# Depthwise convolution taps of a decoder trunk as 32-column products in four column tiles, with host-laid parameters

## The chip, the core and the metric

The kernel runs on one core of one Trainium2 chip. The metric is the time of one execution of the whole program in device microseconds, given as the median of several runs. Before the change it is 1438.3 us (three runs, 1434.78 to 1441.6).

## The reference, cut to what matters

The program is a decoder trunk of four pre-norm residual layers over 256 tokens and 1024 channels, in float32. The token mixer of layer i is attention (layers 0 and 3), a convolution module (layer 1) or a gated recurrence (layer 2). Each layer then has a SwiGLU feed-forward block and a gate by a per-layer embedding p. The change touches the convolution module and the handling of p:

```python
def _conformer_conv(u, w_pw1, b_pw1, w_dw, b_dw, ln_g, ln_b, w_pw2, b_pw2):
    a = u @ w_pw1 + b_pw1                               # 1024 -> 2048
    a = a[..., :CONV_CH] * jax.nn.sigmoid(a[..., CONV_CH:])
    a = causal_depthwise_conv(a, w_dw) + b_dw           # 31 taps, each channel alone
    a = jax.nn.silu(_layernorm(a, ln_g, ln_b))          # over the channels
    return a @ w_pw2 + b_pw2
...
        gate = jax.nn.sigmoid(_rmsnorm(h, ple_norm_g[i]) @ ple_w_gate[i])
        h = h + (p[i] @ ple_w_proj[i]) * gate
```

## The kernel before, in words

A large product has its float32 operands cut into a high and a low part, so it is three products in a reduced float32 type (lines 187 to 189, `mm`). Weights arrive in granules of 128 x 1024 elements (`granule`): a DMA of SyncE's queue fills one of 4 `raw` buffers (line 163), ScalarE writes the high part into one of 9 `whi` buffers (line 166), and VectorE the low part into one of 8 `wlo` buffers (line 167). A scheduler orders the instructions of every engine when the program is built, by the order in which the code names them and by its own estimates; on the chip each queue then runs in that fixed order, SyncE's queue of DMAs too. `issue_after` pins a few instructions behind others.

The convolution (`conv`) holds the channels in eight groups of 128 partitions, with the 256 tokens along the free axis. For each group, pw1 makes 48 products of 256 columns into an `acc` bank, ScalarE takes the sigmoid (line 765), and VectorE the gated product into the tile `glu` (line 768), with 30 zeros ahead of the tokens. The taps then run on two engines. Groups 0 to 4 are chains on VectorE, one instruction for a tap, each reading `glu` shifted by one token and adding to `co` (line 720). Groups 5 to 7 are products on TensorE: for each tap ScalarE scales the identity by the tap's 128 weights (`diag`, line 734), and one float32 product of this 128 x 128 matrix with the shifted `glu` adds to a `mm` bank (line 735). A float32 product shows as two records in the trace, here two of 256 columns.

The statistics are kept relative to `base`, an estimate of the mean from groups 0 and 1. It is subtracted on VectorE, or on TensorE by a product with minus the identity (lines 787 and 796). `moments` (line 751) sums `co` and its square over the channels by products with two columns. When the last group is in, a short chain on VectorE makes 1 / sigma, four products spread it over the partitions (line 822), and each group is normalised, passed through Silu and split into the operand `yT` (lines 830 to 832, 209 and 210). pw2 (`linear`) takes its weights in two halves of 512 columns.

p of each layer is read in two tiles (`pin`), transposed on TensorE and split (`embed_setup`, by `split_T`, line 222), some time before it is needed. `embed` multiplies it by its weights. `conv_setup` reads the convolution's parameters as rows and transposes them on TensorE (lines 680 and 683).

The recurrence of layer 2 holds another use of small tiles: line 970 makes products whose stationary side has 32 or 64 columns, so that their outputs lie in 32 or 64 partitions. With 32 columns the products come in turns for output partitions 0 to 31 and 64 to 95.

Of the kernel before, what the change touches and what calls it, by code (L numbers as in the profile page):

```python
# [16 lines left out]
AF = mybir.ActivationFunctionType  # L17
# [14 lines left out]
TAPS = 31  # L32


def parts(x, n, bits=12):
# [77 lines left out]
class Trunk:  # L113
# [41 lines left out]
    def granule(self, src, nk, n):  # L155
        """src: list of (dram AP [nk*128, cols], first column); hi and lo parts [128, nk, n]"""
# [13 lines left out]
    def ktiles(self, w, cols):  # L170
        """k-tiles (hi, lo) of w[:, cols], where cols: list of (first, count), 256 or 512 in all"""
# [12 lines left out]
    def mm(self, ps, x, w, start, stop):  # L184
        """ps += x.T @ w, float32 operands in two parts each: (hi, lo)"""
# [5 lines left out]
    def mms(self, ps, xs, ws, between=None):  # L191
        """ps = sum of x.T @ w; between() is placed among the products"""
# [10 lines left out]
    def cut(self, x, t, k0=0, k1=None):  # L203
        """k-tiles of an operand for the tokens of tile t (None: all)"""
# [8 lines left out]
    def split_T(self, src, x, k, t):  # L213
        """src [128 tokens of tile t, nk*128] -> k-tiles k.. of the operand x"""
# [13 lines left out]
    def rsqrt(self, ss, scale, w=1):  # L228
        """1 / sqrt(ss * scale + EPS) of [128, w] by Newton's iteration"""
# [24 lines left out]
    def gain(self, row, n=D):  # L254
        """a row of DRAM on all partitions"""
# [31 lines left out]

    def residual(self, t, c, ps):
# [7 lines left out]
    def ffn(self, i, norm, done, pre):  # L296
# [3 lines left out]
        with self.scope(self.nm("ffn")) as pool:  # L300
# [34 lines left out]
            for j in range(NJ):  # L335
# [4 lines left out]
                if j == 5 and i == 0:  # L340
                    self.embed_setup(1)
                    self.embed_setup(2)
                if j == 5 and i == 1:
                    self.embed_setup(3)
# [15 lines left out]
    def embed_setup(self, i):  # L360
        """p transposed and split"""
        pT = self.pT[i] = self.operand(2, "pT", 4)
        for t in range(NT):
            pt = self.tmp("pin", [P, 256], 2)
            self.nc.sync.dma_start(pt, self.a["p"][i, 0, t * P : (t + 1) * P])
            self.split_T(pt, pT, 0, t)
# [42 lines left out]
    def mla_setup(self):  # L409
        """the rotary tables [128, tile, 32]: cos | cos and -sin | sin"""  # L410
# [9 lines left out]
        with self.scope("rope") as pool:  # L420
# [18 lines left out]
            def rounded(x, unit):  # L439
                """x to a multiple of unit (a power of two)"""  # L440
# [53 lines left out]
    def rope(self, x, t, pool):  # L494
        """in place on x [128 tokens, heads, 32]"""
# [14 lines left out]
    def mla(self, i, norm, done, pre):  # L510
# [8 lines left out]
        with self.scope(self.nm("mla")) as pool:  # L519
# [38 lines left out]
            def heads(gi):  # L558
                """q^T, k^T [96, 4, 256], v of four heads"""
# [83 lines left out]
            for gi in range(NH // HG):  # L643
                cur = heads(gi)
                if i == 0 and gi == 0:
                    self.embed_setup(0)
# [13 lines left out]
    def conv_setup(self):  # L660
        nc = self.nc
        a = self.a
        C = self.const
        self.cpar = C.tile([P, KD, TAPS + 3], F32, name="cpar")
        self.cb1 = C.tile([P, 2 * KD], F32, name="cb1")
        self.mean = C.tile([P, P], F32, name="mean")
# [3 lines left out]
        with self.scope("cpar") as pool:  # L670
            rows = self.tmp("rows", [TAPS + 3, D], 1, pool=pool)
            nc.sync.dma_start(rows[:TAPS], a["conv_w_dw"][0])
            for r, k in enumerate(("conv_b_dw", "conv_ln_g", "conv_ln_b")):
                nc.sync.dma_start(rows[TAPS + r : TAPS + r + 1], a[k])
            b1 = self.tmp("b1", [2 * KD, P], 1, pool=pool)
            nc.sync.dma_start(b1, a["conv_b_pw1"][0].rearrange("(c p) -> c p", p=P))
            pt = self.bank("tr", 2)
            n = TAPS + 3
            for c in range(KD):
                nc.tensor.transpose(pt[:, c * n : (c + 1) * n], rows[:, c * P : (c + 1) * P], self.ident[:n, :n])  # L680
            nc.vector.tensor_copy(self.cpar, pt[:, : KD * n].rearrange("p (c n) -> p c n", n=n))
            pt = self.bank("tr", 2)
            nc.tensor.transpose(pt[:, : 2 * KD], b1, self.ident[: 2 * KD, : 2 * KD])
            nc.vector.tensor_copy(self.cb1, pt[:, : 2 * KD])
# [6 lines left out]
    def conv(self, i, norm, done, pre):  # L691
        nc = self.nc
# [3 lines left out]
        PAD = TAPS - 1  # L696
        BASE = 2
        with self.scope(self.nm("conv")) as pool:
# [7 lines left out]
            neg = tmp("neg", [P, P], 1)  # L706
            nc.gpsimd.tensor_scalar(out=neg, in0=self.ident, scalar1=-1.0, scalar2=None, op0=ALU.mult)
# [3 lines left out]
            nc.tensor.matmul(stat[:, : 4 * NT], self.ones, zero, start=True, stop=False)  # L711

            def taps_dve(groups, start):
                """chains of taps; those of a group take turns"""
                for cs in groups:
                    for c, k in cs:
                        if k == 0:
                            start(c)
                        else:
                            V.scalar_tensor_tensor(out=co[:, c], in0=xin[c][:, k : k + S], scalar=par(c, k), in1=co[:, c], op0=ALU.mult, op1=ALU.add)  # L720

            def first(c):
                V.tensor_scalar(out=co[:, c], in0=xin[c][:, :S], scalar1=par(c, 0), scalar2=par(c, TAPS), op0=ALU.mult, op1=ALU.add)

            def first_shifted(c):
                nc.gpsimd.tensor_scalar(out=co[:, c], in0=base, scalar1=-1.0, scalar2=par(c, TAPS), op0=ALU.mult, op1=ALU.add)
                V.scalar_tensor_tensor(out=co[:, c], in0=xin[c][:, :S], scalar=par(c, 0), in1=co[:, c], op0=ALU.mult, op1=ALU.add)

            def taps_pe(c, ps, ks):
                """one diagonal product for each tap"""  # L730
                for k in ks:
                    d = tmp("diag", [P, P], 16)
                    with self.behind():
                        nc.scalar.activation(d, self.ident, AF.Copy, scale=par(c, k))
                    nc.tensor.matmul(ps, d, xin[c][:, k : k + S], start=k == 0, stop=False)  # L735

            def square(c, src, bias=0.0):
                sq[c] = tmp("work", [P, S], 5)
                return nc.scalar.activation(sq[c], src, AF.Square, bias=bias)

            def evict(c, ps):
                nc.scalar.activation(co[:, c], ps, AF.Identity, bias=par(c, TAPS))
                square(c, ps, par(c, TAPS))

            def moments(c):
                """sums over the channels of co (less base) and of its square"""
# [7 lines left out]
            sq = {}  # L754
            xin = []
            for c0 in range(0, KD, 2):
                ws = self.conv_head(i, c0) if c0 else self.head
                for cc in range(2):
                    c = c0 + cc
                    ps = self.acc()  # L760
# [5 lines left out]
                    x = tmp("glu", [P, PAD + S], KD)  # L766
                    nc.gpsimd.memset(x[:, :PAD], 0.0)
                    V.scalar_tensor_tensor(out=x[:, PAD:], in0=ps[:, :S], scalar=self.cb1[:, c : c + 1], in1=sg, op0=ALU.add, op1=ALU.mult)
                    xin.append(x)
            lead = 6  # L770
            taps_dve([[(c, k) for c in (0, 1)] for k in range(TAPS)], first)
            taps_dve([[(2, k)] for k in range(lead)], first)
            pe = {5: self.bank("mm", 2)[:, :S]}
            taps_pe(5, pe[5], range(20))
# [5 lines left out]
            for c in (0, 1):  # L780
# [302 lines left out]
```

## Time and profile before

| | |
|---|---|
| median of three runs | 1438.3 us |
| lowest, highest | 1434.78, 1441.6 us |
| the profiled execution: first to last instruction (span) | 1432.0 us |
| mean granted TensorE clock | 0.991 of full |
| busy share of the span: TensorE, VectorE, ScalarE | 97%, 65%, 51% |
| DMA: bytes, mean rate | 228.90 MB, 160 GB/s |

The profiled execution's own time in the metric is not listed; only its span is. The median of the runs lies 6.3 us over the span: that is what lies around the instructions. In the rows, PE is TensorE's products, PEld its weight loads, DVE VectorE, ACT ScalarE and SPq SyncE's queue. A name like `mm<-glu,diag` says what is written from what.

### The profile page before, as it was taken

The page shows a single profiled execution, that of the slowest core. Times are in us where ns is not written, and L with a number is a line of the kernel's source. Part 1 is how long each engine was busy: PE and PEld are TensorE (multiplying, and loading weights), DVE is VectorE, ACT ScalarE, POOL GpSimd, SP SyncE. Part 2 cuts the span into 40 slices and gives each one's busy share as a digit, 9 for nine tenths or more (in the row PEclk, how much of TensorE's full clock was granted, in tenths as well). Part 3 has the DMA queues.
Part 4 walks back from the last instruction along what each step waited for, and adds up shares of the span by engine and source line. Part 5 has one row for each costly group of instructions (what it writes and reads, how often), then busy time and mean ns, then how long its engine had stood idle before and what let it go on. Part 6 is the DMA issues. An engine that isn't in the chain of part 4 may idle for free.

```text
span 1432.0 us, 19941 instructions
## 1 busy us (share of the span) xinstructions
PE 1382.2 (97%) x7102; PEld 1142.4 (80%) x7102; DVE 933.5 (65%) x1812; ACT 734.0 (51%) x1259; POOL 24.8 (2%) x50
## 2 busy tenths in 40 slices
PE   6999999998999999999989999999999999999996
PEld 5787887876998788888778887887878887788885
DVE  7866555558798865554867767655558867555556
ACT  6665444446655654443554445544445655544443
POOL 0000000001000000000000000000000100000000
PEclk9999999999899999999999999999999999999999
DMA  7433665635630365564573342755535522655532
GB/s 241 167 98 118 200 195 184 194 116 193 213 109 1 120 219 176 180 194 156 160 223 118 124 157 95 240 186 184 191 121 176 195 74 94 209 192 192 186 124 77
DMA packets 172873, 228.90 MB, mean 160 GB/s; under 512 B 11284, under 2 KB 135748, under 8 KB 172774
## 3 DMA queue, kind: packets, MB, share of 16 engines
q1 hardware_dynamic: 172774, 227.63, 49.5%
q8 instruction: 56, 0.92, 0.3%
q14 instruction: 43, 0.35, 0.1%
HBM read 226.53 MB, written 1.05 MB: 159 GB/s over the span
## 4 chain that ended last, share of the span: by engine, by line
PE 75%; DMA 9%; DVE 7%; ACT 6%; issue 3%; SPq 0%; ACTq 0%; DVEq 0%
PE mm L187 12%; PE mm L188 12%; PE mm L189 12%; PE acc L188 8%; PE acc L187 8%; PE acc L189 8%; DMA raw<-in_ffn_w_down_dram 4%; PE tr L222 3%; DVE wlo L167 3%; ACT whi L166 3%; PE mm L735 3%; DMA raw<-in_ple_w_gate_dram 2%; PE acc L957 1%; DMA raw<-in_mla_w_uq_dram 1%; PE acc L604 1%
## 5 line engine op out<-in xcount | busy, mean ns | idle before, releaser
L167 DVE TENSOR_TENSOR wlo<-raw,whi 128x1024 fp32r<-128x1024 f32 (+2 forms) x420 | 498.4, 1200 | 148.9 <-ACT whi L166 105.5
L166 ACT ACTIVATE whi<-raw 128x1024 fp32r<-128x1024 f32 (+2 forms) x420 | 426.8, 1040 | 258.4 <-DMA raw<-in_ffn_w_down_dram 88.6
L187 PE MATMUL mm<-whi,xT 128*128 128x512 f32 x816 | 328.9, 403 | 0.7 <-ACT xT L209 0.4
L189 PE MATMUL mm<-whi,xT 128*128 128x512 f32 x816 | 322.1, 395 | 0.0
L188 PE MATMUL mm<-wlo,xT 128*128 128x512 f32 x816 | 321.7, 394 | 0.0
L189 PEld LDWEIGHTS mm<-whi,xT 128*128 128x128 f32 x816 | 153.5, 188 | 32.7 <-DVE xT L210 0.8
L187 PEld LDWEIGHTS mm<-whi,xT 128*128 128x128 f32 x816 | 153.8, 188 | 30.3 <-ACT xT L209 0.9
L188 PEld LDWEIGHTS mm<-wlo,xT 128*128 128x128 f32 x816 | 153.9, 189 | 28.5
L187 PE MATMUL acc<-whi,aT 128*128 128x512 f32 x352 | 138.7, 394 | 0.6 <-ACT aT L209 0.6
L188 PE MATMUL acc<-wlo,aT 128*128 128x512 f32 x352 | 138.6, 394 | 0.0
L189 PE MATMUL acc<-whi,aT 128*128 128x512 f32 x352 | 136.4, 389 | 0.5 <-DVE aT L210 0.5
L315 DVE SCALAR_TENSOR_TENSOR ga<-mm,rs_y,sg 128x256 f32<-128x256 f32 x88 | 42.3, 481 | 139.0 <-ACT sg L313 139.0
L313 ACT ACTIVATE sg<-mm,rs_y 128x256 f32<-128x256 f32 x88 | 41.0, 465 | 136.6 <-PE mm L189 136.6
L187 PE MATMUL acc<-whi,xT 128*128 128x512 f32 (+2 forms) x272 | 102.2, 380 | 2.2 <-ACT xT L209 1.4
L189 PE MATMUL acc<-whi,xT 128*128 128x512 f32 (+2 forms) x272 | 102.6, 379 | 0.2 <-DVE xT L210 0.2
L188 PE MATMUL acc<-wlo,xT 128*128 128x512 f32 (+2 forms) x272 | 102.2, 377 | 0.0
L187 PEld LDWEIGHTS acc<-whi,aT 128*128 128x128 f32 x352 | 66.1, 188 | 17.5 <-ACT aT L209 3.3
L189 PEld LDWEIGHTS acc<-whi,aT 128*128 128x128 f32 x352 | 66.0, 188 | 16.5 <-DVE aT L210 1.7
L188 PEld LDWEIGHTS acc<-wlo,aT 128*128 128x128 f32 x352 | 66.2, 188 | 13.0
L210 DVE TENSOR_TENSOR aT<-tr,aT 128x256 fp32r<-128x256 f32 x88 | 37.3, 424 | 57.7 <-ACT aT L209 57.7
L720 DVE SCALAR_TENSOR_TENSOR co<-glu,cpar,co 128x256 f32<-128x256 f32 x150 | 60.7, 477 | 0.1
L187 PEld LDWEIGHTS acc<-whi,xT 128*128 128x128 f32 x272 | 51.0, 189 | 11.6 <-ACT xT L209 2.4
(271 smaller groups left out, 1902.4 us busy)
## 6 DMA issues: line engine op xcount, KB each, us to landing
raw<-in_ffn_w_gu_dram SPq DMA_DIRECT2D x352, 256.0 KB, 4.3
raw<-in_ffn_w_down_dram SPq DMA_DIRECT2D x88, 512.0 KB, 4.2
raw<-in_ple_w_gate_dram SPq DMA_DIRECT2D x32, 512.0 KB, 5.2
raw<-in_hgrn_w_in_dram SPq DMA_DIRECT2D x64, 256.0 KB, 4.0
raw<-in_mla_w_out_dram SPq DMA_DIRECT2D x16, 512.0 KB, 4.4
raw<-in_conv_w_pw_dram SPq DMA_DIRECT2D x32, 256.0 KB, 4.8
raw<-in_mla_w_in_dram SPq DMA_DIRECT2D x16, 336.0 KB, 3.4
raw<-in_mla_w_uq_dram SPq DMA_DIRECT2D x12, 384.0 KB, 4.2
```

The lines of the kernel that those rows point to most:

```text
L166: nc.scalar.activation(hi[:, :used], raw[:, :used], AF.Copy)
L167: nc.vector.tensor_tensor(out=lo[:, :used], in0=raw[:, :used], in1=hi[:, :used].bitcast(F32), op=ALU.subtract)
L187: mm(ps, x[0], w[0], start=start, stop=False)
L188: mm(ps, x[0], w[1], start=False, stop=False)
L189: return mm(ps, x[1], w[0], start=False, stop=stop)
L210: v = self.nc.vector.tensor_tensor(out=lo, in0=src, in1=hi.bitcast(F32), op=ALU.subtract)
L222: nc.tensor.transpose(pt[:, (i - k0) * P : (i - k0 + 1) * P], src[:, i * P : (i + 1) * P], self.ident)
L313: nc.scalar.activation(sg, ps[:, :256], AF.Silu, scale=r)
L315: nc.vector.scalar_tensor_tensor(out=ga, in0=ps[:, 256:], scalar=r, in1=sg, op0=ALU.mult, op1=ALU.mult)
L604: nc.tensor.matmul(s1[:, hh], qT[:HD, h, P:], kT[:HD, h], start=True, stop=False)
L720: V.scalar_tensor_tensor(out=co[:, c], in0=xin[c][:, k : k + S], scalar=par(c, k), in1=co[:, c], op0=ALU.mult, op1=ALU.add)
L735: nc.tensor.matmul(ps, d, xin[c][:, k : k + S], start=k == 0, stop=False)
```

## The change

The host lays out four more inputs: p transposed, the convolution's parameters with the channel on the partition, pw1's bias in the same way, and `conv_taps`. Groups 2 and 3 stay chains on VectorE. For the six other groups a group of 128 channels is cut into four blocks j of 32. Four DMAs (`spread`) copy block j of `glu`, SBUF to SBUF, into `win[:, j]`, where a partition is one of 32 channels at one of 4 shifts. A matrix of 128 x 32 with the four taps on its diagonals then does four taps of 32 channels in one product of 256 columns, and its output goes to partitions 32j to 32j+31. Eight steps cover 31 taps, so a group takes 32 products, the four blocks in turns within a step. The matrices come by DMA (`tap_weights`, 512 KB for a group). `win` has three buffers, `tapw` two. The `diag` and `neg` work is gone. pw2 takes its weights by rows of 128 x 1024 (`linear_rows`), five of them named before the last tap groups. p is loaded and split where `embed_weights` is called, which now takes one `raw` buffer more.

```diff
     def embed_weights(self, i):
+        pT = self.pT[i] = self.operand(2, "pT", 2)
+        raw = self.tmp("raw", [P, 1024], 4, pool=self.wpool)[:, : 2 * S].rearrange("p (k n) -> p k n", k=2)
+        self.nc.sync.dma_start(raw, self.a["p_t"][i].rearrange("(k p) n -> p k n", p=P))
+        with self.behind():
+            self.split(*pT, raw)
...
+            def spread(c):
+                win[c] = tmp("win", [P, QUAD, WIN], 3)
+                for j in range(QUAD):
+                    src = xin[c][32 * j : 32 * j + 32]
+                    shifts = bass.AP(tensor=src.tensor, offset=src.offset, ap=[src.ap[0], [1, QUAD], [1, WIN]])
+                    nc.sync.dma_start(win[c][:, j], shifts)
+            def tap_weights(c):
+                tapw[c] = tmp("tapw", [P, QUAD, STEPS, 32], 2)
+                nc.sync.dma_start(tapw[c], a["conv_taps"][:, c])
+            def taps_pe(c):
+                ps = self.bank("mm", 2)[:, :S]
+                for m in range(STEPS):
+                    for j in range(QUAD):
+                        nc.tensor.matmul(
+                            ps[32 * j : 32 * j + 32], tapw[c][:, j, m], win[c][:, j, QUAD * m : QUAD * m + S],
+                            start=m == 0, stop=m == STEPS - 1,
+                        )
+                return ps
...
             for c0 in range(0, KD, 2):
...
+                    if c not in CHAINS:
+                        tap_weights(c)
...
+                    if c not in CHAINS:
+                        spread(c)
+                if c0 == 4:
+                    for c in range(BASE):
+                        nc.scalar.activation(co[:, c], taps_pe(c), AF.Identity, bias=par(c, TAPS))
...
+            for k in range(TAPS):
+                for c in CHAINS:
...
+            self.embed_weights(2)
+            rows = lambda k: self.granule([(a["conv_w_pw2"][0][k * P : (k + 1) * P], 0)], 1, D)
+            ws = [rows(k) for k in range(5)]
+            for c in CHAINS:
+                V.tensor_tensor(out=co[:, c], in0=co[:, c], in1=base, op=ALU.subtract)
+                square(c)
+                moments(c)
+            for c in range(4, KD):
+                V.scalar_tensor_tensor(out=co[:, c], in0=taps_pe(c), scalar=par(c, TAPS), in1=base, op0=ALU.add, op1=ALU.subtract)
+                fence = [square(c).ins]
+                fence.append(moments(c).ins)
...
+    def linear_rows(self, x, ws, use, done, pre):
+        pick = lambda w, c: tuple(y[:, 0, c * 512 : (c + 1) * 512] for y in w)
+        xs = [self.cut(x, t) for t in range(NT)]
+        ps = [self.acc() for c in range(2)]
+        for k in range(KD):
+            for c in range(2):
+                self.mm(ps[c], xs[0][k], pick(ws[k], c), k == 0, k == KD - 1)
...
```

## Rows read from the trace of the kernel before

**Rows 1.** The page: the span, and busy time, share of the span and instructions of two engines.
```profile
span 1432.0 us, 19941 instructions
...
PE 1382.2 (97%) x7102; PEld 1142.4 (80%) x7102; DVE 933.5 (65%) x1812; ACT 734.0 (51%) x1259; POOL 24.8 (2%) x50
```

**Rows 2.** The page: the chain that ended last, share of the span by engine.
```profile
PE 75%; DMA 9%; DVE 7%; ACT 6%; issue 3%; SPq 0%; ACTq 0%; DVEq 0%
```

**Rows 3.** Busy time of each engine in four stretches of the convolution: pw1, taps, statistics, pw2. The numbers behind a stretch are its length, then busy time and records of each engine; after POOL stand the granted clock, the DMA share and GB/s.
```profile
363.00:411.70 48.70, 48.68 (x386) 48.70 (x386) 42.86 (x84) 24.77 (x41) 0.46 (x1) 0.94 0.45 146
411.70:464.00 52.30, 51.74 (x264) 45.52 (x263) 45.04 (x103) 36.12 (x93) 1.51 (x2) 0.97 0.19 61
464.00:474.30 10.30, 9.27 (x36) 6.78 (x36) 7.22 (x32) 4.53 (x10) 0.00 (x0) 0.83 0.01 2
474.30:498.40 24.10, 24.10 (x110) 19.30 (x111) 22.26 (x52) 15.51 (x28) 0.43 (x2) 1.00 0.45 141
```

**Rows 4.** The chain of waits from 411 us on, in order of time: start, us, what (x records).
```profile
411.74 8.64 PE mm L735 x40
...
421.24 8.21 PE mm L735 x38
...
429.87 3.46 PE mm L735 x16
...
435.90 8.27 PE mm L735 x30
444.17 0.43 PE mm L796 x2
444.61 6.91 PE mm L735 x32
...
452.30 6.59 PE mm L735 x30
...
459.36 0.48 ACT co L742
459.88 3.88 PE tr L751 x32
```

**Rows 5.** Line 970 with 32 columns, in stretches of 20 to 35 ns: length, busy time and, in brackets, the records of that line in flight in the stretch; then clock, DMA share and GB/s.
```profile
792.41:792.43 0.02, 0.01 (x2) 1.00 0.25 77
792.43:792.47 0.03, 0.03 (x2) 1.00 0.46 119
792.47:792.49 0.03, 0.03 (x4) 1.00 0.49 123
792.49:792.52 0.03, 0.03 (x6) 1.00 0.66 171
792.52:792.55 0.03, 0.03 (x8) 1.00 0.69 205
```

**Rows 6.** The timeline of TensorE at line 970: start, us from the first start to the last end, line, what (stationary side 128*32 or 128*64), records.
```profile
792.42 0.45 PE L970 MATMUL acc<-qf,kb 128*32 128x32 f32 x16
...
792.80 0.50 PE L188 MATMUL mm<-wlo,xT 128*128 128x512 f32 x1
...
794.50 0.68 PE L970 MATMUL acc<-qf,kb 128*64 128x64 f32 x8
```

**Rows 7.** The timeline of VectorE: the gated product of group 3, taps in a row on two or three chains, and one low part.
```profile
390.06 0.48 DVE L768 SCALAR_TENSOR_TENSOR glu<-acc,cb,work 128x256 f32<-128x256 f32 x1
...
410.91 1.22 DVE L167 TENSOR_TENSOR wlo<-raw,whi 128x1024 fp32r<-128x1024 f32 x1
...
424.79 32.15 DVE L720 SCALAR_TENSOR_TENSOR co<-glu,cpar,co 128x256 f32<-128x256 f32 x81
```

**Rows 8.** The setup on TensorE: the transposes of p as a group, and the timeline around those of the parameters.
```profile
L222 PE MATMUL tr<-ident,pin x16: 270/272/328, 46.6 to 580.4; 128*128 128x128 f32 x16
...
46.65 0.44 PE L222 MATMUL tr<-ident,pin 128*128 128x128 f32 x2 [0.15 <-ACT xT L589]
...
163.51 0.39 PE L189 MATMUL acc<-whi,aT 128*128 128x512 f32 x1
163.83 0.68 PE L680 MATMUL tr<-ident,rows 34*128 34x34 f32 x8
...
164.60 0.50 PE L187 MATMUL mm<-whi,xT 128*128 128x512 f32 x1
```

**Rows 9.** The chain of waits from the gate of layer 0 into the convolution.
```profile
350.96 4.73 DMA raw<-in_conv_w_pw_dram
...
355.78 1.06 ACT whi L166
356.87 1.23 DVE wlo L167
```

**Rows 10.** DMA issues: what, records, KB each, median us from issue to landing; and one issue on SyncE's queue.
```profile
raw<-in_conv_w_pw_dram SPq DMA_DIRECT2D x8, 512.0 KB, 4.9
...
360.98 0.34 SPq L257 DMA_DIRECT2D gain<-in_norm_g_dram  x1
```

**Rows 11.** Around pw2: low parts of its second half, and the high parts of the feed-forward block's first weights.
```profile
476.66 4.62 DVE L167 TENSOR_TENSOR wlo<-raw,whi 128x1024 fp32r<-128x1024 f32 x4
...
490.23 3.89 ACT L166 ACTIVATE whi<-raw 128x1024 fp32r<-128x1024 f32 x4
```

More of the change, by code (lines that the diff above doesn't have):

```diff
@@ L32 @@
 TAPS = 31
+QUAD = 4
 def parts(x, n, bits=12):
@@ L286, in linear @@
         yield
+    def linear_rows(self, x, ws, use, done, pre):
[5 more added lines that the diff above has]
+                self.mm(ps[c], xs[0][k], pick(ws[k], c), k == 0, k == KD - 1)
+        for c in range(2):
+            use(0, c, ps[c])
+        done(0)
+        for c in range(2):
+            ps = self.acc()
+            for k in range(KD):
+                self.mm(ps, xs[1][k], pick(ws[k], c), k == 0, k == KD - 1)
+            use(1, c, ps)
+            del ps
+            if c == 0:
+                pre()
+        done(1)
     def residual(self, t, c, ps):
@@ L669, in conv_setup @@
         nc.gpsimd.memset(self.ones, 1.0)
[L670 to L684, printed above, removed]
     def conv_head(self, i, c0=0):
@@ L711, in conv @@
             nc.tensor.matmul(stat[:, : 4 * NT], self.ones, zero, start=True, stop=False)
[L713 to L735, printed above, removed]
@@ L737, in square @@
-            def square(c, src, bias=0.0):
+            xin, win, tapw, sq = [], {}, {}, {}
+            def spread(c):
[7 more added lines that the diff above has]
+                nc.sync.dma_start(tapw[c], a["conv_taps"][:, c])
@@ L738, in square @@
+            def taps_pe(c):
[7 more added lines that the diff above has]
+                return ps
+            def square(c):
                 sq[c] = tmp("work", [P, S], 5)
-                return nc.scalar.activation(sq[c], src, AF.Square, bias=bias)
@@ L765, in conv @@
                     nc.scalar.activation(sg, ps[:, S:], AF.Sigmoid, bias=self.cb1[:, KD + c : KD + c + 1])
-                    x = tmp("glu", [P, PAD + S], KD)
+                    x = tmp("glu", [P, PAD + S + 2], 4)
                     nc.gpsimd.memset(x[:, :PAD], 0.0)
-                    V.scalar_tensor_tensor(out=x[:, PAD:], in0=ps[:, :S], scalar=self.cb1[:, c : c + 1], in1=sg, op0=ALU.add, op1=ALU.mult)
+                    nc.gpsimd.memset(x[:, PAD + S :], 0.0)
+                    V.scalar_tensor_tensor(out=x[:, PAD : PAD + S], in0=ps[:, :S], scalar=self.cb1[:, c : c + 1], in1=sg, op0=ALU.add, op1=ALU.mult)
                     xin.append(x)
[L770 to L774, printed above, removed]
+                    if c not in CHAINS:
[3 more added lines that the diff above has]
+                        nc.scalar.activation(co[:, c], taps_pe(c), AF.Identity, bias=par(c, TAPS))
             pm = self.bank("tr", 2)[:, :S]
@@ L779, in conv @@
             V.tensor_scalar(out=base, in0=pm, scalar1=KD / BASE, scalar2=None, op0=ALU.mult)
-            for c in (0, 1):
+            for c in range(BASE):
                 V.tensor_tensor(out=co[:, c], in0=co[:, c], in1=base, op=ALU.subtract)
-            taps_pe(5, pe[5], range(20, TAPS))
-            for c in (6, 7):
-                pe[c] = self.bank("mm", 2)[:, :S]
-                taps_pe(c, pe[c], range(8))
-                if c == 6:
-                    nc.tensor.matmul(pe[5], neg, base, start=False, stop=True)
-                taps_pe(c, pe[c], range(8, 16))
-                if c == 6:
-                    for b in (0, 1):
-                        square(b, co[:, b])
-                        moments(b)
-                evict(c - 1, pe[c - 1])
-                moments(c - 1)
-                taps_pe(c, pe[c], range(16, TAPS))
-                nc.tensor.matmul(pe[c], neg, base, start=False, stop=True)
-            evict(7, pe[7])
-            moments(7)
-            order = [[(2, k + lead), (3, k), (4, k)] for k in range(TAPS)]
-            taps_dve([[(c, k) for c, k in g if k < TAPS] for g in order], first_shifted)
-            V.tensor_tensor(out=co[:, 2], in0=co[:, 2], in1=base, op=ALU.subtract)
-            for c in (2, 3, 4):
-                fence = [square(c, co[:, c]).ins]
+                square(c)
+                moments(c)
+            for k in range(TAPS):
+                for c in CHAINS:
+                    if k == 0:
+                        V.tensor_scalar(out=co[:, c], in0=xin[c][:, :S], scalar1=par(c, 0), scalar2=par(c, TAPS), op0=ALU.mult, op1=ALU.add)
+                    else:
+                        V.scalar_tensor_tensor(out=co[:, c], in0=xin[c][:, k : k + S], scalar=par(c, k), in1=co[:, c], op0=ALU.mult, op1=ALU.add)
+            self.embed_weights(2)
[3 more added lines that the diff above has]
+                V.tensor_tensor(out=co[:, c], in0=co[:, c], in1=base, op=ALU.subtract)
+                square(c)
+                moments(c)
+            for c in range(4, KD):
+                V.scalar_tensor_tensor(out=co[:, c], in0=taps_pe(c), scalar=par(c, TAPS), in1=base, op0=ALU.add, op1=ALU.subtract)
+                fence = [square(c).ins]
                 fence.append(moments(c).ins)
@@ L833, in conv @@
                 split = self.split(yT[0][:, c], yT[1][:, c], z)
-                if c == 3:
+                if c in (1, 3, 5):
                     self.fence = split
-                    ws.append(self.ktiles(a["conv_w_pw2"][0], [(512, 512)]))
-            next(self.linear(yT, ws, self.residual, done, pre))
+                    ws.append(rows(len(ws)))
+            self.linear_rows(yT, ws, self.residual, done, pre)
     def hgrn_setup(self):
@@ L1065, in run, with layouts @@
                 self.gate(i, n3, n1.do, lambda: None)
+def layouts(x):
+    w = x["conv_w_dw"][0]
+    steps = (TAPS + QUAD - 1) // QUAD
+    full = np.zeros((steps * QUAD, D), np.float32)
+    full[:TAPS] = w
+    full = full.reshape(steps, QUAD, KD, QUAD, 32)
+    taps = np.zeros((32, QUAD, KD, QUAD, steps, 32), np.float32)
+    for c in range(32):
+        taps[c, :, :, :, :, c] = full[:, :, :, :, c].transpose(1, 2, 3, 0)
+    par = np.concatenate([w, x["conv_b_dw"], x["conv_ln_g"], x["conv_ln_b"]])
+    return {
+        "p_t": np.ascontiguousarray(x["p"][:, 0].transpose(0, 2, 1)),
+        "conv_taps": taps.reshape(P, KD, QUAD, steps, 32),
+        "conv_par": np.ascontiguousarray(par.reshape(TAPS + 3, KD, P).transpose(2, 1, 0)),
+        "conv_b1": np.ascontiguousarray(x["conv_b_pw1"][0].reshape(2 * KD, P).T),
+    }
 def kernel(**inputs):
```

30 lines of the change are left out of this document (7 added, 23 removed).

## The prediction, made before the changed kernel ran

> **What bounds the kernel now.** Read the page's first part before all else: in a span of 1432.0 us TensorE is busy for 97%, VectorE for 65% [rows 1]. The chain that ended last agrees, with 75% of it on TensorE [rows 2]. Then go to the stage that the change rebuilds. In the stretches, pw1 (363.0 to 411.7) keeps TensorE busy for 48.68 of 48.70 us, the taps (411.7 to 464.0) for 51.74 of 52.30, the statistics for 9.27 of 10.30, pw2 for all of 24.10 [rows 3]. VectorE has 45.04 us of work in the tap stretch, so it is close to being a second bound there. The chain of waits through that stretch is almost nothing but line 735, the products with the diagonal matrices [rows 4]: 8.64 + 8.21 + 3.46 + 8.27 + 6.91 + 6.59 = 42.1 us for 186 records. So the convolution ends when TensorE's own work ends, and what counts is how much of that work the change takes away and whether it opens a wait.
>
> **The change part by part.** Durations are those of the profiled execution; the sum is made against its span, 1432.0, and the median of the runs lies 6.3 above it.
>
> Taps on TensorE, removed. The 42.1 us go. A record of 256 columns at full clock takes 8.21 / 38 = 0.216 us [rows 4], so 186 would need 40.2; the other 1.9 us are a piece at half clock (30 records there took 8.27). The three products with minus the identity go too, 3 x 0.43 = 1.3 [rows 4]. Together 43.4.
>
> Taps on TensorE, added. Six groups of 32 products are 192, or 384 records of 256 columns. One after another that is 384 x 0.216 = 82.9 us; with four column blocks side by side 96 x 0.216 = 20.7. Which of the two holds is the main question, and the trace has one place that speaks of it. At line 970 the products with 32 stationary columns lie by turns in two column blocks. Two records are in flight within the first 20 ns, and the count then grows by two every 30 ns or so: 2, 2, 4, 6, 8 [rows 5]. Sixteen records take 0.45 us [rows 6]; less about 0.2 for the last to end, that is 0.25 / 15 = 0.017 us for each. The 64-column products, which lie in one block only, take 0.68 us for eight, which gives (0.68 - 0.2) / 7 = 0.07 each [rows 6], so half as many columns in one block would be 0.035 each. Two blocks thus run fully beside each other. No row shows four, nor 256 columns. I take four, because the pairs start together, and keep both ends: 20.7 and 82.9.
>
> [...] A float32 product is two records on the same block. [...]
>
> Entering and leaving the narrow form costs something. The last pair of line 970 starts near 792.67 and the next wide product at 792.80 [rows 6], some 0.1 us after its columns are through. With both edges I take 0.2 for a group, 1.2 for six; 0 if the edges are free, 3.6 if the scheduler cuts each group into three. So the taps are 20.7 + 1.2 = 21.9 and the step saves 21.5 us.
>
> Taps on VectorE. 155 instructions become 62. In a row they start 32.15 / 81 = 0.397 us apart [rows 7], so the two chains are 24.6 us. Group 3 arrives at about 390.1 [rows 7], group 2 an eighth of pw1 (48.7 / 8 = 6.1) earlier. With the last low parts of pw1 (four, 4.62 [rows 11]), five gated products (2.0) and the work on `base` (1.3) the chains end near 384 + 32.5 = 416.5. Behind them stand seven low parts of the weights for p and pw2, 7 x 4.62 / 4 = 8.1, and only then perhaps the instruction that empties group 4's bank, near 426. TensorE is through with pw1 at 411.7, with groups 0 and 1 (7.3) and the mean at 419.8, and with 4 and 5 at 427. Both `mm` banks are then full, and VectorE comes just in time. I take no wait; 0 to 8.
>
> Waits that the change adds. The matrices of group 6 need the buffer of group 4: 0.34 us of issue and 4.9 to land [rows 10] after group 4 ends, in which TensorE has group 5 (3.65) and sums of 0.96 (8 of the 32 records in 3.88 [rows 4]) to do. That leaves 0.6 to 1.6, and as much for group 7: I take 1.5 for both, 0 to 3.3. Behind these DMAs on SyncE's queue stand weights of p and pw2, which TensorE wants only after the statistics, more than 10 us later. The copies of the last group wait for its gated product: two instructions of 0.48, four issues of 0.34 and a landing that I take like a weight's, some 7 us; groups 4 and 5 cover it (7.3). Without that cover it would be seen whole. The copies and matrices of groups 0 and 1 are due 20 us after they can start.
>
> The end of the taps. Before, 0.48 us of ScalarE stood between the last product and the sums, which then took 3.88 [rows 4]. Now the last group needs 0.48 on VectorE, 0.42 for its square and its own sums of 0.96, while the other groups' sums can go ahead. I take +0.8, 0 to 1.5.
>
> The setup. Sixteen transposes of p go; two in a pair start 0.44 - 0.27 = 0.17 us apart [rows 8], which would be 2.7, and since neighbours overlap I take 2.0 (0 to 2.7). The transposes of the parameters push the next product from 163.51 + 0.22 to 164.60, 0.9 us [rows 8]. All of it lies among products of a bound TensorE. Saved: 2.9.
>
> The gate of layer 0. `embed_weights` for the convolution now takes a third `raw` buffer of four, so one granule of pw1 more is loaded after the gate's weights let go. There the chain is a DMA of 4.73, a high part of 1.06 and a low part of 1.23 [rows 9], before the norm's chain goes on. One granule more is at least its ScalarE time, 1.06, and at most the DMA's again. Against it, the split of p in four pieces goes. I take +1.5, -1 to +4. In layers 0, 2 and 3 the same call stands ahead of long stretches of products and costs nothing.
>
> pw2 by rows. Three instead of four low parts fall among the normalisations [rows 11], 1.15 us less on an engine that is not the bound. Against it the buffers of the rows come free only during the last quarter of pw2, and the feed-forward block's first high parts (3.89 for four [rows 11]) start later. I take 0; -1 to +2.
>
> The clock. The stretch from 464.0 has 0.83 [rows 3] of full, and the half-clock piece of the taps is counted as gained above. Any wait in the new order may bring such a piece back: I take +1, 0 to 3.4.
>
> The sum: -21.5 + 1.5 + 0.8 - 2.9 + 1.5 + 1.0 = -19.6. The span would be 1412.4 and the time 1412.4 + 6.3 = 1418.7, say **1419 us**.
>
> **The rivals.** *Neighbours only.* If the order of records is strict, the first of a block waits for the second of the block before: 192 x (0.216 + 0.006) = 42.6 us, with the edges 43.8, against 43.4 before. The waits then vanish under longer groups, and -2.9 + 0.8 + 1.5 remain: 1438. For it: no row shows more than two blocks at once. Against it: the even counts [rows 5].
>
> *One block at a time.* The slower side: four streams of 256 float32 columns can't be read or added up together, so the groups take 82.9 us. Then 82.9 + 1.2 - 43.4 = +40.7, less 2.9 and plus 2.3: 1478. It decides from the point where the blocks overlap less than about twofold (43.4 / 82.9). For it: the products that overlap in the trace have 32 columns, not 256. Against it: they do so without any loss.
>
> *The copies become the bound.* The four DMAs of a group and its matrices, through a queue that runs in order and two buffers, come later than TensorE wants them, about 5 us for each of groups 6 and 7, and the half clock follows: 1419 + 10 = 1429. For it: two `tapw` buffers and 4.9 us to land. Against it: TensorE has other groups to do meanwhile.
>
> **How the numbers follow.** The forecast has 0.70, the copies 0.08, neighbours only 0.12, one block at a time 0.10. A measurement of this kernel can tell about 0.5%, 7.2 us, from no change. The forecast and the copies are faster by more than that: 0.78; neighbours only is the same: 0.12; one block at a time is slower: 0.10. The forecast's own range, with the bounds of its terms taken together in part, is 1410 to 1428. Up to 1440 it also takes in the copies and the neighbours and leaves one block at a time out.
>
> **What would show it.** In the page of the changed kernel the products `mm<-win,tapw` should be 384 records, and a group of 64 should take about 3.5 us on the timeline; 7 would be neighbours only, 14 one block at a time. Groups 6 and 7 should wait at most 2 us each for `tapw`. The sums should end near 443 instead of 463.8, and the two chains on VectorE near 417. TensorE should show no records of `diag`, `neg`, `pin` or `rows`. The prediction is wrong if a group takes more than 5 us, if VectorE's chains end after TensorE has finished groups 4 and 5, or if the way from the gate of layer 0 to pw1 grows by more than 4 us.

## The result, and the profile after

The changed kernel takes 1422.7 us (median of four runs, 1418.08 to 1426.17) against 1437.5 for the kernel before in the same comparison: ratio 0.990, 95% interval 0.9872 to 0.9927. It is faster by 14.8 us, 1.0%, in the range and 3.7 us over the forecast. Term by term two errors stand behind that, and they partly cancel.

The page of the changed kernel (profiled run 1418.08 us) answers to [rows 1, 2]:

```profile
span 1416.3 us, 20148 instructions
...
PE 1368.3 (97%) x7269; PEld 1120.7 (79%) x7269; DVE 897.8 (63%) x1718; ACT 702.0 (50%) x1161; POOL 24.9 (2%) x55
...
PE 73%; DMA 9%; DVE 9%; ACT 5%; issue 3%; SPq 0%; DVEq 0%; ACTq 0%
```

TensorE still sets the time. The span is 15.8 us shorter, but TensorE's busy time only 13.9, though 42 us of diagonal products went and the new tap products should take about half of that. Stretches of the convolution, with the columns of [rows 3], show why:

```profile
360.80:415.90 55.10, 55.10 (x512) 51.95 (x511) 44.94 (x85) 20.57 (x27) 0.62 (x8) 0.96 0.67 198
415.90:423.10 7.20, 4.08 (x56) 2.10 (x54) 5.28 (x9) 2.84 (x5) 0.00 (x0) 1.00 0.97 331
423.10:440.20 17.10, 17.06 (x114) 11.43 (x110) 2.84 (x3) 2.73 (x7) 0.00 (x0) 0.50 0.33 105
440.20:453.40 13.20, 12.15 (x173) 7.46 (x166) 1.45 (x3) 2.35 (x4) 0.00 (x0) 1.00 0.35 122
```

The first row is pw1 with the taps of groups 0 and 1 inside it; the others are the taps of groups 4 to 7 and the sums, which are the two-column products of `moments`. The sums end at 453.4, where the prediction had 443. In the second TensorE works for 4.08 of 7.20 us. In the third it is busy all the time (17.06 of 17.10 us) at a granted clock of 0.50 and gets through 114 records; the fourth, at full clock, has 173 in 13.2. The busy share hides this; the clock column shows it. The timeline of TensorE and then of ScalarE (start, us, line, what, records, and in brackets the idle time before and what ended it) tells where the hole comes from:

```profile
416.49 2.35 PE L732 MATMUL mm<-win,tapw 128*32 128x256 f32 x34
421.96 0.38 PE L748 MATMUL tr<-mean,co 128*128 128x2 f32 x2 [3.12 <-DVE co L779]
```

```profile
409.98 0.48 ACT L762 ACTIVATE work<-acc,cb 128x256 f32<-128x256 f32 x1 [5.45 <-PE acc L190]
415.24 1.06 ACT L167 ACTIVATE whi<-raw 128x1024 fp32r<-128x1024 f32 x1 [4.78 <-DMA raw<-in_conv_w_pw_dram]
418.40 1.06 ACT L167 ACTIVATE whi<-raw 128x1024 fp32r<-128x1024 f32 x1 [2.11 <-DMA raw<-in_conv_w_pw_dram]
419.36 0.46 ACT L762 ACTIVATE work<-acc,cb 128x256 f32<-128x256 f32 x1
```

The last group of pw1 ends at about 415.7, and its sigmoid (line 762) could run then. But ahead of it in ScalarE's queue stand two high parts of pw2's rows, which wait 4.78 and 2.11 us for their transfers, and it starts behind them, at 419.36. The chain of waits goes on from there:

```profile
413.27 5.05 DMA raw<-in_conv_w_pw_dram
...
419.36 0.47 ACT work L762
...
420.63 0.48 DVE glu L766
421.11 0.34 DVE base L777
...
421.48 0.44 DVE co L779
...
421.96 0.38 PE tr L748 x2
```

On VectorE a low part of 1.23 us comes between the sigmoid and the last gated product, and `base` stands behind that product; the sums of group 0 wait for `base`, and on TensorE the rest of the tap groups stands behind these sums. So a transfer that pw2 wants 40 us later holds TensorE for 3.12 us (the hole, below), and the clock falls 1.1 us behind it, at 423.1.

Theory A: these conversions, named too early, cost the wait and, through the hole, the clock: some 3.1 us and, as an estimate, half of 17.1, 8.5. Theory B: VectorE or the transfers of the tap weights bound the stage anyway. Theory C: not the hole, but the alternation of narrow tap pieces and two-column sums keeps the clock low.

### The profile page after: what moved, and what is told of

Its sections match the earlier page's. It is cut to its first block, busy times and chain, and to the rows that moved or that the text cites. A ratio compares the mean times of both kernels' runs of the same rounds, so it can differ in the third digit from the quotient of the medians.

```text
span 1416.3 us, 20148 instructions
## 1 busy us (share of the span) xinstructions
PE 1368.3 (97%) x7269; PEld 1120.7 (79%) x7269; DVE 897.8 (63%) x1718; ACT 702.0 (50%) x1161; POOL 24.9 (2%) x55
## 4 chain that ended last, share of the span: by engine, by line
PE 73%; DMA 9%; DVE 9%; ACT 5%; issue 3%; SPq 0%; DVEq 0%; ACTq 0%
PE mm L188 13%; PE mm L189 13%; PE mm L190 13%; PE acc L189 7%; PE acc L188 7%; PE acc L190 7%; DVE wlo L168 4%; DMA raw<-in_ffn_w_down_dram 4%; PE tr L223 3%; ACT whi L167 3%; DMA raw<-in_ple_w_gate_dram 2%; DVE co L787 1%; PE mm L732 1%; PE acc L949 1%; PE acc L619 1%
## 5 line engine op out<-in xcount | busy, mean ns | idle before, releaser
L188 PEld LDWEIGHTS acc<-whi,aT 128*128 128x128 f32 x352 | 66.1, 188 | 17.1 <-ACT aT L210 2.8
L190 PEld LDWEIGHTS acc<-whi,aT 128*128 128x128 f32 x352 | 66.1, 188 | 15.8 <-DVE aT L211 1.0
L188 PEld LDWEIGHTS acc<-whi,xT 128*128 128x128 f32 x272 | 51.1, 189 | 10.3 <-ACT xT L210 1.3
L190 PEld LDWEIGHTS acc<-whi,xT 128*128 128x128 f32 x272 | 51.2, 188 | 8.3 <-DVE xT L211 0.8
```

The lines of the kernel that those rows point to most:

```text
L188: mm(ps, x[0], w[0], start=start, stop=False)
L190: return mm(ps, x[1], w[0], start=False, stop=stop)
```

## The experiments

All were timed against the kernel before, which had medians of 1433.6 to 1435.3 us in these comparisons and 1437.5 in that of the changed kernel; ratios are to it. A difference to the changed kernel is therefore better taken from the ratios (0.990 for the changed kernel) than from the medians.

**Conversions behind the last gated product.**

```diff
+            self.fence = [sgi.ins, glui.ins]
             self.embed_weights(2)
```

`sgi` and `glui` are the last group's sigmoid and gated product.

> The conversions of the next embedding's weights and of the first five rows of the second pointwise product are issued behind the last group's sigmoid and its gated product; nothing else is changed. Theory A (these conversions, waiting for their transfers, hold up the last sigmoid; from that come TensorE's 3.1 us wait at 418.8 us and the 17.1 us at half clock behind it, which cost about 8.5 us): the wait goes, the sums end at 441 to 445 us in place of 453.2, and the time is 8 to 12 us under the changed kernel's 1422.7, about 1412. Theory B (VectorE, or the transfers of the tap weights, bound the stage anyway): within 2 us of 1422.7. Theory C (the clock falls because narrow pieces of taps and two-column products alternate, whatever the wait): the wait goes, the half clock stays, about 1419.5.

Measured: 1410.3 us, ratio 0.9842 (0.9815 to 0.9869): 12.4 us under the changed kernel by the medians, 8.3 by the ratios. The stretches from 360.8 on:

```profile
360.80:414.00 53.20, 53.20 (x511) 50.06 (x512) 42.27 (x82) 16.81 (x23) 1.17 (x9) 1.00 0.66 197
414.00:442.00 28.00, 26.52 (x327) 16.49 (x326) 12.82 (x18) 11.80 (x18) 0.00 (x0) 1.00 0.76 230
```

The sums end at 442.0, the clock is 1.00 throughout, and narrow pieces and sums alternate as before. From the first tap record of group 4 to the last sum it is 27.2 us, against 36.9 in the changed kernel (416.5 to 453.4): 9.7 less. A holds, B and C as stated fall. The profile is of one execution: another of the six took 1417.97 us at a mean granted clock of 0.987, as low as the changed kernel's 0.985 to 0.988, so without this hole the clock can still fall; where it fell there, no trace shows.

**Whole tap groups.** Sums are issued only between groups: those of groups 0 to 3, 32 records, behind group 4, the others behind the next group.

```diff
+                with self.tc.issue_after(tail[c].ins):
+                    for b in due:
+                        last = moments(b).ins
```

> The two-column products of the sums are issued only between whole tap groups (behind the last product of group 4, 5, 6 and 7), so that no group is cut; the conversions stay where they were. Theory A: the last sigmoid is as late as before and TensorE waits as long, now behind the whole of group 4; the clock falls again: within 3 us of 1422.7. Theory C: the pieces are whole, the clock stays at its upper level from 423 us on or falls for 3.4 us only: 5 to 8 us less, about 1416. Theory B: within 2 us of 1422.7.

Measured: 1415.9 us, ratio 0.9877 (0.9853 to 0.9901). The median is the one that C gave, but by the ratios it is only 3.3 us under the changed kernel, about A's limit of 3. Two stretches, and a row of TensorE's timeline, speak against C's reason:

```profile
417.10:421.60 4.50, 0.04 (x4) 0.00 (x0) 2.96 (x5) 1.42 (x2) 0.00 (x0) 1.00 1.01 323
421.60:435.30 13.70, 11.44 (x76) 9.00 (x80) 4.43 (x8) 3.54 (x7) 0.00 (x0) 0.50 0.60 211
...
422.27 0.59 PE L748 MATMUL tr<-mean,co 128*128 128x2 f32 x2 [5.12 <-DVE co L779]
```

TensorE stands still for 5.12 us, and 4.5 us into that the clock falls, with not one narrow piece cut. It comes back after 13.7 us, not 17.1. What whole groups are worth besides shows further down.

**Both.**

```diff
+            self.fence = [sgi.ins, glui.ins]
...
+                with self.tc.issue_after(tail[c].ins):
```

> Both edits: conversions behind the last gated product, and whole tap groups. Theory A: as the first edit alone, about 1412, within 2 us of it. Theory C: only this one has both the wait and the half clock gone: about 1411 where the first edit alone gives 1419.5. Theory B: within 2 us of 1422.7.

Measured: 1411.2 us, ratio 0.9844 (0.982 to 0.9867), as the first edit alone. But the hole was back in another place. The chain:

```profile
416.83 4.79 DMA raw<-in_conv_w_pw_dram
...
421.63 0.02 ACT whi L167
...
422.60 0.41 ACT work L740
...
423.05 3.15 PE tr L748 x14
```

```profile
414.00:421.70 7.70, 7.50 (x93) 5.32 (x91) 6.16 (x10) 4.51 (x8) 0.00 (x0) 1.00 0.59 179
421.70:431.90 10.20, 8.85 (x70) 5.84 (x74) 2.85 (x3) 3.08 (x5) 0.00 (x0) 0.50 0.66 219
```

Now the square of a group (line 740) stands behind a conversion. TensorE does sums from 419.2 on and stands still from 421.65 to 423.05; the clock falls at 421.7 for 10.2 us. It falls when this hole of 1.4 us is not 0.1 us old, so here the hole can hardly be what brought it down; 18 records of sums stood ahead. That whole groups, which save time elsewhere, make up for this is argued, not shown.

**The hole filled.** The kernel with whole groups, and 56 full-width products whose result nobody uses behind group 4.

```diff
+                        for k in range(56):
+                            last = nc.tensor.matmul(full, xs[0][0][:, :P], xs[0][0], start=True, stop=True)
```

> The kernel with whole tap groups, the conversions where the change put them, and 56 full-width products (128x256 of an operand that lies ready, their result is used nowhere) between the products of group 4 and the first sums: they fill the stretch from 417 to 424 us in which TensorE had nothing to do. VectorE's and ScalarE's wait is untouched. If TensorE's idle stretch is what brings the clock down (theory A, its second half): the clock stays at 1.00 behind the filling, the 28 us of sums and taps that follow at 0.50 for 13 us shrink by some 6 us: the sums end at 441 to 443 us (448.2 without the filling), the time is 4 to 6 us under the 1415.9 of the kernel without it, about 1411. If the thin products bring it down (theory C): the clock falls behind the filling as before, within 2 us of 1415.9, or up to 2 us over it by the filling itself.

Measured: 1413.3 us, ratio 0.9857 (0.9822 to 0.9891), 2.6 us less than without the filling, where 4 to 6 were expected; the two intervals overlap. The sums end at 446.9, not at 441 to 443. The chain and the stretch at half clock:

```profile
419.92 6.91 PE acc L801 x56
426.82 3.47 PE tr L748 x32
430.29 5.28 PE mm L732 x64
```

```profile
415.40:430.90 15.50, 15.50 (x171) 13.23 (x172) 11.46 (x17) 6.02 (x10) 0.00 (x0) 1.00 0.93 308
430.90:434.30 3.40, 3.40 (x37) 1.73 (x33) 0.00 (x0) 0.00 (x0) 0.00 (x0) 0.50 0.91 330
```

The fall shrinks from 13.7 to 3.4 us, so the hole caused most of it. But one is left, without a hole: it comes at 430.9, 0.6 us behind 32 records of sums in a row. Hence theory A': a hole, or a long row of two-column products, brings the clock down. Three runs tested the row.

**Filling, sums spread:** 16 records behind each of groups 4 to 7.

```diff
-                    for b in due:
+                    for b in ((0, 1), (2, 3), (4, 5), (6,))[c - 4]:
```

> The kernel with the filling (56 full-width products whose result is used nowhere), and the sums of the first groups no longer 32 products' records in a row behind it but 16 behind each of the groups 4 to 7; as many products in all. In the kernel with the filling the clock fell at the end of that row, for 3.4 us. Theory A': TensorE idle or a row of two-column products of 3 us and more brings the clock down: it stays at 1.00 through the tap groups, the sums end 1.7 us sooner than there (445.0 from 446.7, shifted by the start of the stage), 1411.5 against its 1413.3. Theory D (the fall there has nothing to do with the row): a fall of 3.4 us or more again between 425 and 445 us, 1413 to 1414.

Measured: 1412.8 us, ratio 0.9853 (0.983 to 0.9876). No fall before the sums end:

```profile
425.30:443.50 18.20, 18.20 (x258) 13.32 (x258) 1.80 (x4) 2.07 (x4) 0.00 (x0) 1.00 0.34 115
```

The clock does as A' says, and not in the profile alone: the mean granted clock of the six executions is 0.993, against 0.990 with 32 in a row. The time, 0.5 us less, can't tell, since single runs differ by more.

**Sums gathered, no hole:** conversions behind the squares of groups 0 to 3, groups 4 and 5 in a row, then 40 records of sums.

```diff
+            self.fence = [late, glui.ins]
             self.embed_weights(2)
...
+                    for b in ((), (0, 1, 2, 3, 4), (5,), (6,))[c - 4]:
+                        last = moments(b).ins
```

> Conversions behind the last gated product and the squares of groups 0 to 3, whole tap groups, groups 4 and 5 in a row, and behind them the sums of groups 0 to 4 in one row, 40 records, some 4.9 us; TensorE should not be idle ahead of them. The counterpart of the first edit, where at most eight such records stand in a row and the clock stayed at 1.00. Theory A': the clock falls during or right behind the row, for 3.4 us or more (1.7 us or more lost): 1412 to 1414 against the first edit's 1410.3. Theory A alone (only idle TensorE brings it down): 1.00 throughout, 1409 to 1411, sums end at 441 to 443 us.

`late` is the square of group 3. Measured: 1408.1 us, ratio 0.9814 (0.9791 to 0.9837). Chain and stretch:

```profile
416.69 7.04 PE mm L732 x128
423.74 6.46 PE tr L748 x40
430.20 4.93 PE mm L732 x64
```

```profile
423.70:426.10 2.40, 2.40 (x26) 2.40 (x22) 1.76 (x3) 1.36 (x2) 0.00 (x0) 1.00 0.97 316
426.10:432.90 6.80, 6.80 (x48) 5.37 (x51) 0.78 (x2) 0.42 (x1) 0.00 (x0) 0.50 0.97 336
```

TensorE is busy to the last hundredth, and the clock falls 2.4 us into the row, as A' says. The time alone would speak for A alone: it is under the 1412 to 1414 that A' gave and just under A's 1409 to 1411. I had left out that whole groups save time at full clock as well, as the next run shows. The 128 tap records ahead of the row can't be needed for the fall: with the filling it came behind 56 full-width products and 32 records of sums.

**Sums spread, no hole, no filling.**

```diff
-                    for b in ((), (0, 1, 2, 3, 4), (5,), (6,))[c - 4]:
+                    for b in ((0, 1), (2, 3), (4, 5), (6,))[c - 4]:
```

> As the kernel that gathered the sums (conversions behind the squares of groups 0 to 3, whole tap groups), with the sums of two groups, 16 records, behind each of the tap groups 4 to 7 in place of 40 in a row. Theory A' (a long row of two-column products or an idle TensorE brings the clock down): no fall until the sums have ended; the 6.8 us at half clock that the row cost there are worth 3.4 us: 1404 to 1406 against its 1408.1, sums ending at 438 to 439 us. Rival: the squares of groups 0 and 1 are not ready when group 4 ends, TensorE waits 1 us or more and the clock falls for that: 1408 or more.

Measured: **1403.9 us** (1403.57 to 1408.07), ratio 0.9802 (0.9782 to 0.9821), the lowest median of all. Its interval overlaps that of the run before (0.9791 to 0.9837), so the times alone don't part the two; the mean clocks are 0.9924 and 0.991, and the traces do. Its chain has nothing but TensorE in it, and its stretch no fall:

```profile
415.61 3.59 PE mm L732 x64
419.20 1.88 PE tr L748 x16
421.07 3.59 PE mm L732 x64
...
435.60 1.95 PE tr L748 x16
437.55 0.23 PE tr L806 x2
```

```profile
415.60:437.80 22.20, 22.20 (x324) 15.71 (x324) 12.74 (x18) 11.59 (x17) 0.00 (x0) 1.00 0.72 235
```

The same work takes the first edit 414.8 to 442.0, 27.2 us, also at 1.00. So cutting the groups, with the order of the sums that goes with it, costs 5.0 us by itself: three waits, 1.4 us together, for a group's sums right behind it, and the edges of the pieces.

Against the changed kernel this one has 18.8 us less by the medians, of which 3.9 lie between the kernels before of the two comparisons; by the ratios it is some 14. The traces say 14.7 for the stretch from group 4 to the last sum (36.9 and 22.2). The terms one by one, 3.1 (hole), 8.5 (half of 17.1) and 5.0 (cutting), add to 16.6, so they overlap by some 2 us; how, was not tried.

**Blocks one after the other.** For the main question of the prediction, what lets four blocks run side by side:

```diff
-                for m in range(STEPS):
-                    for j in range(QUAD):
+                for j in range(QUAD):
+                    for m in range(STEPS):
```

> Within a tap group the four 32-channel blocks come one after the other (eight products of a block, then the next block), in place of turns between the blocks; the products are the same. If only neighbours in the program's order can run side by side: a group takes four times its 3.45 us, 13.8 us, six groups cost 62 us more, about 1480 us. If products of different column blocks also pass others that wait: a group stays at about 3.5 us and the time within 3 us of 1422.7. If a neighbour at the change of block alone overlaps: between 1470 and 1480.

Measured: 1453.7 us, ratio 1.0138 (1.0098 to 1.0178), slower than before the change; none of the three forecasts, 1480, 1470 to 1480 and 1423, is met. Records of line 732 in flight, first in the kernel above with turns, then here in stretches over a change of block (a record lasts 0.379, one block starts one every 0.216):

```profile
415.80:415.86 0.06, 0.06 (x8) 1.00 0.99 189
```

```profile
461.68:461.80 0.12, 0.12 (x2) 1.00 0.92 376
461.90:462.02 0.12, 0.12 (x3) 1.00 1.24 512
462.12:462.24 0.12, 0.12 (x4) 1.00 1.24 512
462.34:462.45 0.11, 0.11 (x4) 1.00 0.84 344
462.55:462.66 0.11, 0.11 (x4) 1.00 0.93 363
...
463.00:463.13 0.13, 0.13 (x2) 1.00 1.05 370
```

Two in flight is one block, four are two blocks, eight all four. In strict order the next block could run beside this one only while the last record of this one lasts, 0.379 us at most; here four are in flight in all three stretches from 462.12 to 462.66. At each change four records of the next block run beside the last four of this one, so a block takes 12 steps of 0.218, 2.6 us, and not 16, and a group 10.5 us with its edges left out. The overlap reaches four records across and no further: the turns in the program's order are needed.

**pw2's weights by column halves**, with the first edit.

```diff
-            ws = [rows(k) for k in range(5)]
+            ws = [self.ktiles(a["conv_w_pw2"][0], [(0, 512)])]
...
-            self.linear_rows(yT, ws, self.residual, done, pre)
+            next(self.linear(yT, ws, self.residual, done, pre))
```

> Conversions behind the last gated product, as in the first edit, but the second pointwise product keeps its weights in two column halves, as in the kernel before (linear in place of linear_rows; half the weights are converted behind the fourth split). It measures what the rows are worth by themselves. The prediction put them at 0 (-1 to +2): then 1409 to 1412, as the first edit's 1410.3. A rival: with column halves the second half's weights come late and the product waits for them: 2 to 5 us over, 1412 to 1415.

Measured: 1409.3 us, ratio 0.9825 (0.9791 to 0.9859), as the first edit's 0.9842. The rows are worth nothing that can be told from an interval of 4.9 us each way, and the rival's 1412 to 1415 is not seen.

**The host-laid part alone**, in the kernel before.

```diff
+        nc.sync.dma_start(self.cpar, self.a["conv_par"])
+        nc.sync.dma_start(self.cb1, self.a["conv_b1"])
...
+        self.nc.sync.dma_start(raw, self.a["p_t"][i].rearrange("(k p) n -> p k n", p=P))
+        with self.behind():
+            self.split(*pT, raw)
```

> The kernel before with p, the convolution's parameters and biases laid out by the host and loaded by plain transfers; taps and second pointwise product as in the kernel before. It measures the host-laid part alone. The prediction's terms for it are -2.9 for the setup and +1.5 for the first gate: -1.4 against the kernel before. The cumulative difference of the two traces up to the first gated product, -3.2, says: -3 to -4 by its arrival, if nothing later gives it back.

Measured: 1427.0 us, ratio 0.9952 (0.993 to 0.9974), some 6.9 us, more than the 3 to 4 expected. In its trace the convolution, from the first gated product to the first one of the feed-forward block behind it, lasts 131.8 us, as before (131.3).

## Why the prediction was right, and where not

*Taps on TensorE.* Right. Four blocks run side by side: 64 records take 3.59 us [rows 4: 0.216 for one], against 3.65 forecast with its edges. 384 records of `mm<-win,tapw` are there, and the even counts at two blocks [rows 5], which strict order would not give, did speak for four. One after another the 64 would take 64 x 0.216 = 13.82 us; 13.82 / 3.59 = 3.85, 0.96 of four.

*The edges* hold for whole groups. But the scheduler cut the groups, and the 5.0 us that this costs the four last ones in the first edit's kernel, 1.4 of waits in it, are over the 3.6 which I had as the end for six; in the changed kernel the cost was not measured by itself.

*Taps on VectorE, no wait.* The chains end at 415.5, as forecast (416.5). The wait came all the same, 3.12 us, within the range of 0 to 8 but by ScalarE. I had counted the low parts that stand in VectorE's queue, but not asked where the high parts would come in ScalarE's. The change names five rows of weights ahead of the last tap groups; two of their high parts stood in ScalarE's queue ahead of the sigmoid and waited 4.78 and 2.11 us for their transfers.

*The clock.* This is the step that failed: +1 with an upper end of 3.4. It was some 8.5 us, an estimate, half of 17.1. The later fall, 3.4 us from 453.8, is no addition: the kernel before has one as long at the same place, behind its sums [rows 3: 0.83]. I took the pieces of 3.4 us that the kernel before shows [rows 3, 4] as the largest that can come, though its 0.94 over the 48.7 us of pw1 [rows 3] already means 5.8 us at half clock, the end of a fall of 10.2 us. The kernels here had stretches of 3.4 (before), 6.8 (sums gathered), 10.2 (both edits), 13.7 (whole groups) and 17.1 us (the change) at half clock.

*Waits for `tapw`.* None, where 1.5 was forecast. The waits of TensorE from 411 to 455 name only VectorE's `co` (us in total, times, longest):

```profile
PE tr L748 <- DVE co L779: 3.1, 1, 3.1
PE tr L748 <- DVE co L796: 0.9, 3, 0.6
```

In the fastest kernel tap groups and sums follow each other without a gap. The copies don't bound either.

*Setup and gate.* Forecast -2.9 + 1.5 = -1.4; alone the part is worth 3.7 to 10.0 us by its interval. In the two traces 4.1 us of it go in the feed-forward block of layer 0, where the transposes of p and of the parameters stood; the rest is in small steps up to the end. Why it is more than the transposes' own time was not tried. The gate is not where the sum went wrong: from its transposes to the first product of pw1 it is 18.85 us after the change and 17.90 before, +0.95 where +1.5 was forecast.

*pw2 by rows.* Forecast 0, measured nothing that can be told.

Together, the convolution between the same two events (first gated product to the first one of the feed-forward block) was to gain 18.2 us (-21.5 + 1.5 + 0.8 + 1.0). It gained 8.7 in the changed kernel, 20.0 with the first edit and 23.4 in the fastest. The 1419 came near because 10 us too few for hole and clock met some 5 too few for the host-laid part: that it came so near is luck, the mechanism of the taps is not. The whole gain was to be 19.6 us; it is 14.8, by its interval 10.5 to 18.4. The 6.3 us that the sum adds are not what lies around the instructions: a run's time is about 1.8 us over its own span (1418.08 and 1416.3), and the rest is that the profiled execution was faster than the median. The gain doesn't hang on it.

*The rivals.* Neighbours only and one block at a time fall by the 3.59 us. How the records run with blocks one after the other speaks against strict order as well: the next block's first record starts while earlier ones of this block still wait.

## What to carry to other kernels

Naming pw2's rows early also queued their conversions early, ahead of the sigmoid (4.78 and 2.11 us of waiting in ScalarE's queue): look in each engine's queue for an instruction that waits for a transfer ahead of one on the path, and pin it behind. Count the hole not by its length alone but with the clock behind it; here 3.1 us of waiting cost some 8.5 more, an estimate. Keep narrow products that run side by side in whole groups (cutting them cost 5.0 us here), and spread products of few columns between these groups (40 records in a row cost 6.8 us at half clock, 16 none).

## What the runs showed of the hardware

- The clock fell at a busy share of 100%: 2.4 us into a row of 40 two-column records (for 6.8 us), and 0.6 us behind a row of 32 (for 3.4 us), but not with 16 in a row between tap groups. Each of these is one profiled execution; the mean clocks over all executions go the same way: 0.991 and 0.990, against 0.9924 and 0.993.
- Whole tap groups of 32 stationary columns, four blocks side by side, 64 records in 3.59 us, ran at 1.00 for 22.2 us, with 16 sums behind each group (415.6 to 437.8 in the fastest kernel).
- With blocks one after the other, records started out of the program's order: four of the next block ran beside the last four of the block before (four in flight in all three stretches from 462.12 to 462.66, where one lasts 0.379 us). So the fixed order that the description of the kernel before gives to every queue did not hold for the starts of TensorE's records there.
- The stretch at half clock ahead of pw1 is 10.2 us long in the profiles of before (from 358.2) and after (from 354.8). Their pages have 8 for the clock in that slice of the 40; the pages of eight of the experiments have 9 there, though the code up to there is that of the changed kernel. Of eleven runs of the kernel before in one comparison, the two with the highest mean clock, 0.994 and 0.995, were the fastest (1427.3 and 1428.9 us, median 1435.3), which fits a part of the clock in what single runs differ by.
